# W_G's weight sums in the middle block's W_O, column sums by transposition, and four smaller edits to a one-core layer kernel

## The chip, the core and the metric

The kernel runs on one core of one Trainium2 chip. The core has five engines, each with an in-order queue of its own: TensorE (PE; its weight loads are listed as PEld), VectorE (DVE), ScalarE (ACT), GpSimd (POOL) and SyncE (SP), which here only issues transfers. Sixteen DMA engines carry all transfers, whether SP or POOL issued them. The metric is the device time of one execution, in microseconds. Before the change it is 2609.93, the median of three runs (2609.04 to 2610.62).

## What is computed

One layer over 2048 prompt tokens and 64 decode tokens, 1024 wide. The projections go into a short convolution (path A) and a recurrence over 8 heads in chunks of 64 tokens (path B); both are gated, merged and multiplied by `w_o`; a norm, a residual, another norm and a gate follow. Cut to what matters:

```python
h = rms_norm(x, g_pre)
vA, bA, cA, zA, q, f, iv, zB, gA, gB = split_cols(einsum('btd,dn->btn', h, w_in))
u = cA * vA
yA = einsum('btc,cd->btd', silu(zA) * bA * causal_conv3(u_ext, conv_w), w_a_out)
S_new, o = hgrn2_scan(S0, silu(q) * QK_SCALE, 1 - fg, iv, log(fg))   # chunks of 64
yB = einsum('btc,cd->btd', rms(o) * g_onorm * silu(zB), w_b_out)
out = einsum('btd,de->bte', sigmoid(gA) * yA + sigmoid(gB) * yB, w_o)
x = x + rms_norm(out, g_post)
gate = sigmoid(einsum('btd,de->bte', rms_norm(x, g_ple), w_ple_gate))
x = x + einsum('btp,pd->btd', p, w_ple_proj) * gate
```

`rms_norm` divides each token by the root of the mean of its squares over the 1024 features. All is fp32.

## The kernel before

**Layout.** Features lie on the 128 partitions, tokens along the free axis. The 2112 tokens are cut into three blocks of 704 (`BN`), each of two halves of 352 (`HN`). A feature row block is a tile of 128 x 704 from one ring of 52 such buffers (`RING`, tag "r", `rt()`); half tiles come from nine "hf" buffers (`hf()`). The ring serves almost everything: x, operands, heads, outputs, weights that are being summed. PSUM has five banks for gemms and three for the rest.

**Arithmetic.** Each fp32 operand is split into a high half (a cast on ScalarE, `split`) and a low half (a subtraction on VectorE), and each product takes three matmuls: high by high, high by low, low by high (L363 to L365 in `sgroup`, L496 to L498 in `in_turn`, L529 to L531 in `mm3`). A weight block of 128 x 512 needs a raw buffer (5), a high buffer (4, tag "hi", `split_w`) and a low one (4 "lo" or 3 "s"). Low halves that were made once are kept in DRAM and loaded again.

**Seven products.** Pairs of output row blocks are computed for both token halves with seven products of block sums instead of eight (`PRODUCTS`, `sgroup`); the weights need four sums, S1 to S4, for each pair. In block 0 they are made as needed (`combined`, L297). For W_A, W_B, W_O and W_G `prepare_sums` makes them ahead: for each of four pairs POOL loads four blocks into ring tiles, VectorE makes four sums (L337 to L343), ScalarE and VectorE split them, and POOL stores the sums and their low halves (L326, L329), to be loaded again by SP when they are used. The token side needs sums too (`operands`: x is loaded by POOL at L643, scaled at L693, summed at L675 to L678 and split).

**Order.** The framework lays out each engine's queue at compile time by priority and readiness as it estimates them, except where `issue_after`, `high_priority` or a "hook" says otherwise. `hooks` is a list of small steps: after each of the seven products of a group (and each half gemm) one is taken, so that a head's attention (`head_attn`, four steps per part, three parts) or a norm (`final_norm`) is threaded into the products. An entry None lets a product pass. `spread_out` builds such a list for the norms; it must be used up by the groups that follow (seven groups of seven products).

**Stages of a block.** Gates and path B (eight heads; `path_b`), path A (`path_a`, with `side` running the next block's column norms and a `prepare_sums`), the merge (W_A, W_B), W_O, and the final norm, which runs by hooks inside the next block's first gates. At the end of W_O the next block's operands are made (`ops`, in steps 1, 3, 5 and 7 of `final_out`). The second block's output gate with W_G (`final_gate`) is done inside the last block, for which its rows are stored and loaded again; the last block uses the seven products for W_G as well (`gate_in_turn`), and there W_G's sums are read.

**The norms.** `col_rstd` sums squares over the 128 partitions: for each 128 tokens a matmul with the squares as weights and a column of ones as the moving operand (L620), then scale (VectorE, L591) and power (POOL, L593). `spread` turns the three columns back by transposition against the identity (L604), and a copy takes them out of PSUM (L630).

Of the kernel before, what the change touches and what calls it, by code (L numbers as in the profile page):

```python
# [18 lines left out]
P = 128  # L19
D = 1024  # L20
# [15 lines left out]
CUT = 1344  # L36
BN = 704
HN = BN // 2
NB = TOK // BN
RING = 52  # L40
# [5 lines left out]
def plan():  # L46


    out = []
    for t0 in range(0, TOK, BN):  # L50
        runs, groups = [], []
        for lo, hi, sample in ((0, CUT, False), (CUT, CUT + DEC, True), (CUT + DEC, TOK, False)):
            a, b = max(lo, t0) - t0, min(hi, t0 + BN) - t0
# [7 lines left out]
        halves = [dict(t0=t0 + o, off=o, n=HN) for o in (0, HN)]  # L61
        out.append(dict(t0=t0, n=BN, runs=runs, npair=npair, parts=parts, groups=groups, segs=halves, last=t0 + BN == TOK))
# [20 lines left out]
def hybrid_step(  # L83
# [34 lines left out]

    def rt(n=BN, dt=F32):
        t = ring.tile([P, BN + 4], dt, tag="r", name=nm("r"))  # L120
        return t if n is None else t[:, :n]

    def hf(n=HN):
        return ring.tile([P, HN + 32], F32, tag="hf", name=nm("hf"), bufs=HALVES)[:, :n]

# [3 lines left out]
    def ps_gemm():  # L129
        return psg.tile([P, 512], F32, tag="pg", name=nm("pg"))[:, :HN]  # L130

    def spill(kind, j):
        return dram.tile([P, BN], F32, tag=f"{kind}{j}", name=nm(kind), bufs=2)
# [4 lines left out]
    ones = const.tile([P, 1], F32, tag="ones", name="ones")  # L138
    V.memset(ones, 1.0)
# [6 lines left out]
    keep = const.tile([P, BN], F32, tag="keep", name="keep")  # L146
    atts = [
        const.tile([P, max(len(b["parts"][i]) for b in blocks), P], F32, tag=f"att{i}", name=f"att{i}") for i in range(NPART)
# [41 lines left out]
    def split_rt(src):  # L190
        hi, lo = rt(dt=F32R), rt(dt=F32R)
        split(src, hi, lo)
        return hi, lo
# [19 lines left out]
    def split_w(raw, key=None, queue=SP):  # L213

        hi = wp.tile([P, 4, P], F32R, tag="hi", name=nm("hi"))
# [178 lines left out]
    def half(t, h):  # L394
        return t[:, h * HN : (h + 1) * HN]
# [151 lines left out]
    def gemm_late(idxs, act, segs, late):  # L547
# [3 lines left out]
        ks = [k for k in range(KB) if k != late] + [late]  # L551
# [55 lines left out]
    def spread_all(cols):  # L607

        rs = rt()
        for h in range(2):  # L610
            A.copy(half(rs, h), spread(cols[h], HN))
        return rs

    def col_rstd(acc, n):
# [3 lines left out]
        with placed():  # L618
            for i, o in tiles_of(n):
                T.matmul(pc[:, i : i + 1], acc[:, o : o + P], ones, start=True, stop=True)  # L620
        rstd_of(pc[:, : cols.shape[1]], cols, 1.0 / D)
# [19 lines left out]
    def load_x(bl, k):  # L641
        t = rt()
        G.dma_start(t, x_fm[k * P : (k + 1) * P, bl["t0"] : bl["t0"] + BN])  # L643
        return t

    def row_rstd(bl, out):

        out.extend(cols_tile(HN) for _ in bl["segs"])
        todo = [(cols, s["t0"] + o, i) for cols, s in zip(out, bl["segs"]) for i, o in tiles_of(HN)]
# [120 lines left out]
    def path_a(bl, hc, a, first, extra, ready=None):  # L770

        for j in range(KB):
            next(extra, None)
            n = bl["n"]
            pos = [r[0] + 2 * i for i, r in enumerate(bl["runs"])]
            hists = [hist_s if r[2] else hist_p for r in bl["runs"]]
            ct, u, conv = rt(), rt(None), rt()
# [4 lines left out]
            def times_u(h, v):  # L782
                for (o, ln, _), q in zip(bl["runs"], pos):
                    lo, hi = max(o, h * HN), min(o + ln, (h + 1) * HN)
                    if lo < hi:
                        V.tensor_tensor(
                            u[:, q + 2 + lo - o : q + 2 + hi - o], v[:, lo - h * HN : hi - h * HN], ct[:, lo:hi], ALU.mult
# [13 lines left out]
            for (o, ln, _), q, hist in zip(bl["runs"], pos, hists):  # L801
                d = conv[:, o : o + ln]
                A.mul(d, u[:, q : q + ln], cw[0][:, j : j + 1])
                for w in (1, 2):
                    V.scalar_tensor_tensor(d, u[:, q + w : q + w + ln], cw[w][:, j : j + 1], d, ALU.mult, ALU.add)
# [20 lines left out]
    def head_prep(bl, hc, hd, first, hs):  # L826
        n, npair = bl["n"], bl["npair"]
        nch, np1 = n // CH, npair * P
# [18 lines left out]
        qc = small.tile([P, 2, BN // CH], F32, tag="qc", name=nm("qc"))  # L847
        f, r = qc[:, 0, :nch], qc[:, 1, :nch]
        ka, kb, qx, vt, z = hf(HN + 32), rt(), rt(), rt(), rt()

        def scaled(after):
# [16 lines left out]
            two = kb[:, : 4 * P].rearrange("p (c q t) -> p c q t", q=4, t=CH)  # L868
            rest = kb[:, 4 * P : np1].rearrange("p (g c t) -> p g c t", c=2, t=CH)[:, :, 0, :]

            def pairs(x, at):
                return x[:, : 4 * P].rearrange("p (c e h t) -> p c e h t", e=2, h=2, t=CH)[:, :, :, at, :]
# [629 lines left out]
```

## Time and profile before

| | |
|---|---|
| median of 3 runs | 2609.93 us |
| profiled execution | 2611.61 us |
| its span, first to last instruction | 2609.9 us |
| TensorE busy in the span | 2588.6 us |
| TensorE clock granted (mean) | 1.000 |
| bytes moved by DMA | 745.99 MB, 286 GB/s over the span |

In a list of waits a row reads: engine, tile and line that waited, what it waited for, then us in total, times, longest. In the chain of waits a row is start, us, what ran (or was waited for) on the chain that ended last. In the timeline a row is start, duration, engine, line, operation, tiles, shape, and in brackets the idle time before it with what ended it. In a table of stages a row is from:to, length, then busy us and instruction count of PE, PEld, DVE, ACT, POOL, the clock, the DMA share and GB/s. In a list of groups: line, engine, operation, out<-in, shapes, count | busy us, mean ns | idle before. In the list of transfers the last number is the median time in us from issue to landing. TensorE's matmuls overlap, so starts lie closer together than durations: a 352-column matmul is listed with about 0.32 us and the next starts 0.16 us later.

### The profile page before, as it was taken

How to read it: one execution, taken by the hardware profiler on the slowest of the kernel's cores; microseconds unless marked ns; L12 is line 12 of the kernel's file. 1: busy time of each engine (PE TensorE's matmuls, PEld its weight loads, DVE VectorE, ACT ScalarE, POOL GpSimd, SP SyncE). 2: the span in 40 equal slices, each digit the busy share in tenths (PEclk: the TensorE clock that was granted, in tenths of full speed). 3: DMA queues.
4: the chain of work that ended last, by engine and by line, in shares of the span. 5: the costliest groups of instructions: out<-in, count | busy, mean ns of one | idle time of the engine just before them, and what ended most of it. 6: DMA issues, size and time to landing. Idle time of an engine off the chain costs nothing.

```text
span 2609.9 us, 47443 instructions
## 1 busy us (share of the span) xinstructions
PE 2588.6 (99%) x16562; PEld 2572.5 (99%) x16562; DVE 1667.1 (64%) x3232; ACT 1538.9 (59%) x2940; POOL 392.6 (15%) x722
## 2 busy tenths in 40 slices
PE   8999999999999999999999999999999999999999
PEld 8999999999999999999999999999999999999998
DVE  8778888888766555455545568553455544568756
ACT  6666665554434644677745556466667744555746
POOL 2000000200441212101112211021000101210220
PEclk9999999999999999999999999999999999999999
DMA  7687787898988997777789989599776789999977
GB/s 285 234 275 259 251 285 257 306 318 286 342 292 285 351 320 259 248 231 224 226 288 359 381 311 312 193 359 358 229 230 220 224 256 335 377 321 309 339 256 240
DMA packets 362672, 745.99 MB, mean 286 GB/s; under 512 B 44640, under 2 KB 49280, under 8 KB 362432
## 3 DMA queue, kind: packets, MB, share of 16 engines
q1 hardware_dynamic: 319680, 579.55, 65.4%
q0 software_dynamic: 42464, 163.37, 17.0%
q8 instruction: 130, 2.13, 0.3%
q14 instruction: 110, 0.90, 0.1%
q10 hardware_dynamic: 288, 0.05, 0.0%
HBM read 531.74 MB, written 211.04 MB: 285 GB/s over the span
## 4 chain that ended last, share of the span: by engine, by line
PE 89%; DMA 3%; DVE 2%; issue 2%; ACT 1%; POOL 1%; DVEq 0%; POOLq 0%; ACTq 0%; SPq 0%
PE pg L363 19%; PE pg L365 19%; PE pg L364 19%; PE pg L496 4%; PE pg L497 4%; PE pg L498 4%; PE pg L530 4%; PE pg L531 4%; PE pg L529 4%; PE pa L994 1%; PE pa L958 1%; PE pa L996 1%; PE pa L944 1%; DMA r<-w_blk 1%; DMA raw<-S 1%
## 5 line engine op out<-in xcount | busy, mean ns | idle before, releaser
L363 PE MATMUL pg<-r,hi 128*128 128x352 f32 x3304 | 1092.9, 331 | 4.6 <-DVE r L409 3.1
L364 PE MATMUL pg<-r,hi 128*128 128x352 f32 x3304 | 1067.6, 323 | 0.0
L365 PE MATMUL pg<-r,lo 128*128 128x352 f32 x2356 | 762.1, 323 | 1.2 <-DMA lo<-low 1.2
L218 ACT CAST hi<-raw 128x512 fp32r<-128x512 f32 x720 | 445.0, 620 | 499.8 <-PE pg L364 165.6
L363 PEld LDWEIGHTS pg<-r,hi 128*128 128x128 f32 x3304 | 622.2, 188 | 9.1 <-DVE r L409 3.2
L364 PEld LDWEIGHTS pg<-r,hi 128*128 128x128 f32 x3304 | 622.2, 188 | 0.0
L365 PEld LDWEIGHTS pg<-r,lo 128*128 128x128 f32 x2356 | 442.3, 188 | 1.8 <-DMA lo<-low 1.7
L365 PE MATMUL pg<-r,s 128*128 128x352 f32 x948 | 306.2, 323 | 0.1
L530 PE MATMUL pg<-r,hi 128*128 128x352 f32 x768 | 248.4, 324 | 0.0
L529 PE MATMUL pg<-r,hi 128*128 128x352 f32 x768 | 248.1, 323 | 0.0
L188 ACT CAST hi<-raw 128x512 fp32r<-128x512 f32 x218 | 134.6, 621 | 153.1 <-PE pg L364 53.5
L188 DVE TENSOR_TENSOR r<-r,r 128x352 fp32r<-128x352 f32 (+3 forms) x298 | 182.8, 637 | 62.7 <-ACT r L188 61.7
L497 PE MATMUL pg<-r,hi 128*128 128x352 f32 x672 | 217.3, 325 | 0.0
L496 PE MATMUL pg<-r,hi 128*128 128x352 f32 x672 | 213.6, 325 | 0.1
L531 PE MATMUL pg<-r,lo 128*128 128x352 f32 x656 | 211.9, 323 | 0.1
L188 ACT CAST r<-r 128x352 fp32r<-128x352 f32 (+3 forms) x298 | 162.2, 580 | 56.9 <-DVE r L1114 15.4
L188 DVE TENSOR_TENSOR lo<-raw,hi 128x512 fp32r<-128x512 f32 x218 | 149.4, 687 | 63.5 <-ACT hi L188 55.2
L365 PEld LDWEIGHTS pg<-r,s 128*128 128x128 f32 x948 | 178.4, 188 | 0.4 <-DMA s<-low 0.4
L188 ACT CAST hi<-s 128x512 fp32r<-128x512 f32 x160 | 98.5, 621 | 123.0 <-PE pg L364 105.8
L377 ACT COPY hf<-pg 128x352 f32<-128x352 f32 x354 | 157.1, 446 | 11.5 <-PE pg L365 10.9
L530 PEld LDWEIGHTS pg<-r,hi 128*128 128x128 f32 x768 | 144.3, 188 | 0.3 <-DVE r L188 0.2
L529 PEld LDWEIGHTS pg<-r,hi 128*128 128x128 f32 x768 | 144.2, 188 | 0.0
(367 smaller groups left out, 4157.0 us busy)
## 6 DMA issues: line engine op xcount, KB each, us to landing
raw<-w_blk SPq DMA_DIRECT2D x570, 256.0 KB, 4.2
lo<-low SPq DMA_DIRECT2D x411, 256.0 KB, 4.4
raw<-S SPq DMA_DIRECT2D x408, 256.0 KB, 4.4
low<-lo SPq DMA_DIRECT2D x314, 256.0 KB, 3.7
s<-low SPq DMA_DIRECT2D x309, 256.0 KB, 4.2
S<-s SPq DMA_DIRECT2D x152, 256.0 KB, 3.2
r<-w_blk POOLq DMA_DIRECT2D x64, 256.0 KB, 7.3
S<-r POOLq DMA_DIRECT2D x64, 256.0 KB, 5.8
```

Source lines behind the costliest of these rows:

```text
L188: return A.copy(hi, src).ins, V.tensor_tensor(lo, src, hi.bitcast(F32), ALU.subtract).ins
L218: A.copy(hi, raw)
L363: add(hi[:, k, :], xhi, start=start and k == 0, stop=False)
L364: add(hi[:, k, :], xlo, start=False, stop=False)
L365: last[0] = add(lo[:, k, :], xhi, start=False, stop=k == KH - 1).ins
L377: copied = A.copy(got[n], ps[bank])
L496: add(hi[:, k, :], xhi, start=start and k == 0, stop=False)
L497: add(hi[:, k, :], xlo, start=False, stop=False)
L498: last[0] = add(lo[:, k, :], xhi, start=False, stop=k == KH - 1).ins
L529: T.matmul(ps, hi[:, k % 4, :], xhi[:, c], start=k == ks[0], stop=False)
L530: T.matmul(ps, hi[:, k % 4, :], xlo[:, c], start=False, stop=False)
L531: last[0] = T.matmul(ps, lo[:, k % 4, :], xhi[:, c], start=False, stop=k == ks[-1]).ins
```

## The change

- `prepare_sums((W_G,), ...)` runs in the middle block, in steps 0, 2, 3, 4 and 5 of `final_out` (the first only loads), and no longer in the last block's `path_a`.
- `col_rstd` transposes the squares (three transposes into PSUM) and lets VectorE add up along the free axis; the column of ones goes.
- The high halves of weights have five buffers instead of four; the ring has 51 tiles instead of 52.
- The last block's two half norms share their three working tiles and load x once, in whole rows.
- `final_gate` keeps the sigmoid in half tiles, multiplies in place and loads x in the step that uses it.
- One more empty hook before the last attention step of block 0's first head; in `spread_out` for the first two blocks' norm one more empty hook before each spreading and one fewer behind the last row of the norm's first pass.
- `gemm_late` takes k in the order late+1, ..., late (mod 8) instead of 0, 1, ... with `late` at the end.
- Block sizes come from a list, `SIZES = (704, 704, 704)`. The blocks, their halves and the attention's parts stay as they were; the helpers take the width from the current block (`wide`, `width_of`, `of_block`).

The core of the diff, without the edits that only rename widths:

```diff
-RING = 52
+RING = 51
...
-        hi = wp.tile([P, 4, P], F32R, tag="hi", name=nm("hi"))
+        hi = wp.tile([P, 4, P], F32R, tag="hi", name=nm("hi"), bufs=5)
...
-        ks = [k for k in range(KB) if k != late] + [late]
+        ks = [(late + 1 + k) % KB for k in range(KB)]
...
             for i, o in tiles_of(n):
-                T.matmul(pc[:, i : i + 1], acc[:, o : o + P], ones, start=True, stop=True)
-        rstd_of(pc[:, : cols.shape[1]], cols, 1.0 / D)
+                T.transpose(pc[:, i * P : i * P + P], acc[:, o : o + P], ident)
+        nt = cols.shape[1]
+        V.tensor_reduce(cols, cols3(pc, nt), axis=mybir.AxisListType.X, op=ALU.add)
+        rstd_of(cols, cols, 1.0 / D)
...
-                    hooks.append(None)
+                    hooks.extend([None] * (2 if first and hd == 0 else 1))
...
-    def final_norm(bl, segs, xo, acc, h2, kept, raw=False):
+    def final_norm(bl, segs, xo, acc, h2, kept, raw=False, common=None):
+        common = {} if common is None else common
+        if not common:
+            common.update(tiles=[rt(), rt(), rt()], xks=[])
...
-        acc2, rs, rs2 = rt(), rt(), rt()
-        xks = []
-        def fetch():
-            j = len(xks)
-            if j < KB:
-                xks.append(rt())
-                G.dma_start(xks[j][:, c], x_fm[j * P : (j + 1) * P, segs[0]["t0"] : segs[0]["t0"] + n])
-        for _ in range(3 if bl["last"] else 4):
-            fetch()
+        (acc2, rs, rs2), xks = common["tiles"], common["xks"]
+        ahead = 3 if bl["last"] else 4
+        def fetch(upto):
+            while len(xks) < min(upto, KB):
+                xks.append(load_x(bl, len(xks)))
+        fetch(ahead)
...
     def final_gate(bl, segs, h2, kept, queue=G):
-        def fetch(j):
-            return [reload(kept[kind, j]) for kind in "xp"] if j < KB else None
-        nxt = fetch(0)
+        nxt = reload(kept["p", 0])
         for j in range(KB):
+            pj, xj = nxt, reload(kept["x", j])
             pss = gemm(W_G + j, h2, segs)
-            (xj, pj), nxt = nxt, fetch(j + 1)
-            t = rt()
+            nxt = reload(kept["p", j + 1]) if j + 1 < KB else None
             for s, ps in zip(segs, pss):
-                A.activation(t[:, cols_of(s)], ps, AF.Sigmoid)
-            V.tensor_tensor(t, pj, t, ALU.mult)
-            V.tensor_tensor(t, t, xj, ALU.add)
+                gate = hf()
+                A.activation(gate, ps, AF.Sigmoid)
+                V.tensor_tensor(pj[:, cols_of(s)], pj[:, cols_of(s)], gate, ALU.mult)
+            V.tensor_tensor(pj, pj, xj, ALU.add)
...
-        sums_ahead = prepare_sums((W_A, W_B), True) if first else prepare_sums((W_O,) if nxt else (W_G,), False)
+        sums_ahead = prepare_sums((W_A, W_B), True) if first else prepare_sums((W_O,), False) if nxt else iter(())
+        gate_sums = prepare_sums((W_G,), False) if nxt and not first else iter(())
...
             for j, _ in enumerate(final_out(segs, mg, xo, acc, KB - 1 if first else KH - 1)):
+                if j in (0, 2, 3, 4, 5):
+                    next(gate_sums, None)
                 if j in (1, 3, 5, 7):
                     run(ops, 1)
...
-            spread_out((norm, (0, 1, 0, 1) + (0, 1, 0) * KB + (0, 1, 0, 1) + (0, 1) * KB))
+            spread_out((norm, (0, 1, 0, 0, 1) + (0, 1, 0) * (KB - 1) + (0, 1) + (0, 1, 0, 0, 1) + (0, 1) * KB))
```

170 lines of the change are left out of this document (97 added, 73 removed).

## The prediction

> **What bounds the kernel now.** I read the page first (busy time, clock), then who TensorE waited for, then a table of stages, then the chain of waits and the timeline at the places that the change touches.
>
> ```profile
> span 2609.9 us, 47443 instructions
> PE 2588.6 (99%) x16562; PEld 2572.5 (99%) x16562; DVE 1667.1 (64%) x3232; ACT 1538.9 (59%) x2940; POOL 392.6 (15%) x722
> PEclk9999999999999999999999999999999999999999
> ```
>
> TensorE (PE) is busy for 99% of the span, at the full clock in every slice. Only two kinds of gain are left: TensorE work taken out, and the 21 us (2609.9 - 2588.6) in which it idles. What it waited for, in total, times and longest, in us:
>
> ```profile
> PE pa L1058 <- ACT r L188: 6.6, 1, 6.6
> PE pg L363 <- DVE r L409: 3.1, 9, 0.6
> PE pa L1008 <- DVE r L1003: 1.7, 1, 1.7
> PE pg L363 <- ACT hi L218: 1.5, 2, 0.7
> PE pg L365 <- DMA lo<-low: 1.2, 1, 1.2
> ```
>
> The first is the start of the program, which the change leaves. The second, third and fourth are what three of its edits aim at, 6.3 us together. The fifth, one late weight, isn't addressed. So no edit can bring much, and each is counted in single microseconds.
>
> **Column sums by transposition.** `col_rstd` runs 14 times: twice at the start, then four times for each block. Today each sends 3 matmuls against a column of ones, which appear as 6 TensorE instructions (84 in all); afterwards 3 transposes, such as L604 already runs. The chain of waits shows both, as start, us, what:
>
> ```profile
> 858.00 1.44 PE pa L620 x12
> 862.12 0.66 PE pa L604 x6
> 906.99 1.23 PE pa L620 x12
> 1705.02 1.47 PE pa L620 x12
> 1752.76 1.23 PE pa L620 x12
> 2455.18 0.56 PE pa L620 x6
> ...
> 2485.12 0.56 PE pa L620 x6
> 2509.59 0.80 PE pa L620 x6
> ```
>
> These rows, with a third one of 0.56 left out, are the twelve calls of the three final norms (x12 is two calls, one for each half): 1.44 + 1.23 + 1.47 + 1.23 + 3 x 0.56 + 0.80 = 7.85 us. Six transposes take 0.66, so 0.11 each; 12 x 3 x 0.11 = 3.96. That is **-3.9 us**, on a TensorE with nothing idle around it. The two calls at the start are taken at nothing: there VectorE sets the pace (below). The ends are -3.4 (0.80 and the two 1.4s contain waits that stay) and -4.6 (the start gains its 0.7 too).
>
> ```profile
> L604 PE MATMUL pa<-ident,cols x54: 270/272/324, 24.3 to 2514.2; 128*128 128x128 f32 x54
> ```
>
> This row gives 0.272 us as the duration of a transpose by itself; 0.11 holds only where the next one starts inside it. [...]
>
> Each call also gains a VectorE reduction over 128x384, 14 in all:
>
> ```profile
> L1001 DVE TENSOR_REDUCE ms<-r 128x4 f32<-128x512 f32 x24 | 16.5, 686 | 30.5 <-ACT r L1000 30.5
> 25.18 0.53 DVE L1354 COPY r<-pa 128x352 f32<-128x352 f32 x1 [0.58 <-PE pa L604]
> ```
>
> 384/512 of 0.686 is 0.51 us. In the two norms of the first two blocks it is covered, because the list of hooks gets one more empty step between the sums and the spreading: one product, 12 matmuls, 1.9 us. In the last block the next step comes a whole half-gemm later (24 matmuls, 3.9 us). At the start two of them, 1.0 us, meet 0.58 us of idle VectorE, and the transposes end 0.7 us sooner. So nothing; if the cover is gone, 0.5 us each, 14 x 0.5 = 7 us at most.
>
> **Spread later.** In the first head of the first block the transposition at L1008 comes before VectorE has finished L1003 (start, us, what):
>
> ```profile
> 124.32 0.63 DVE r L1003
> 125.08 0.63 PE pa L1008 x4
> 125.71 0.16 PE pg L365
> 127.45 0.30 PE pa L1008
> ```
>
> 1.7 us of idle (the row of waits above), 0.63 instead of 4 x 0.11 for the restart, and 0.3 more at 127.45, where the second part's transposition arrives early as well. One more empty hook puts L1008 behind 12 further matmuls, 12 x 0.16 = 1.9 us; the data is there at 124.95. **-2.2 us**; ends -2.2 and -1.0 (VectorE, in a queue of its own order, slips with it). What follows, the store of that head's z, comes a product later, and its reader is block 0's merge, after all eight heads.
>
> **A fifth buffer for high halves.** The first group of gates of a block interleaves four products by k, and so holds four high halves until its end. The fifth product's cast can't start before:
>
> ```profile
> 850.04 0.17 PE pg L365
> 850.58 0.63 ACT hi L218
> 851.26 0.43 PE pg L363
> ```
>
> It happens twice (the row of waits). Each costs 0.74 us of idle plus 0.27 (0.43 - 0.16) of restart. With a fifth buffer the cast is done during the four products. **-2.0 us**; ends -2.0 and 0 (if the cast stays queued on ScalarE behind the copy that precedes it). Six of the nine waits of L363 for L409 are in block 0, one in each of six heads, and this is the first:
>
> ```profile
> 180.40 0.43 PE L363 MATMUL pg<-r,hi 128*128 128x352 f32 x1 [0.25 <-DVE r L409]
> ```
>
> There VectorE's low halves for the sums stand ahead of the copy that frees a PSUM bank. ScalarE casts one product earlier with the fifth buffer, so VectorE's order there may change either way: 0, ends -3.1 (six of 0.25 + 0.27) and +1.5 (six idle times doubled).
>
> **W_G's sums.** They leave the middle of the last block and enter W_O of the middle block: 16 loads, 16 sums, 16 splits and 32 stores. The stages (us, PE, PEld, DVE, ACT, POOL, clock, DMA share, GB/s):
>
> ```profile
> 1340.00:1510.00 170.00, 169.40 (x1053) 169.13 (x1053) 86.30 (x170) 94.11 (x196) 41.59 (x93) 1.00 0.99 358
> 1596.00:1698.00 102.00, 101.47 (x627) 99.76 (x625) 60.71 (x112) 54.95 (x110) 6.44 (x12) 1.00 0.67 231
> 2130.00:2290.00 160.00, 158.98 (x985) 158.46 (x985) 75.75 (x125) 78.76 (x150) 27.94 (x58) 1.00 0.98 346
> ```
>
> The second row is where they go, the third where they come from; the first has W_O's own sums. In the third, TensorE twice waits behind VectorE, which waits for the weights loaded by POOL and then does three sums ahead of the copy that TensorE needs:
>
> ```profile
> 2198.71 9.26 DMA r<-w_blk
> 2210.86 0.69 DVE r L343
> 2211.55 0.44 DVE r L409
> 2212.13 0.40 PE pg L363
> 1677.62 1.07 POOL L643 DMA_DIRECT2D r<-x_fm  x2 [28.36 <-PE pg L531]
> ```
>
> Of the 3.1 us in nine waits, six of 0.25 belong to block 0; the three left, 1.6 us, are 0.53 each, and 0.24 of restart (0.40 - 0.16) makes 0.77. Two of them are W_G's: -1.5. In the new place VectorE gets 32 operations of 0.69, 22 us on 60.7 of 102; ScalarE 16 casts of about 0.63, 10 us; POOL 48 issues of 0.54 (half of the L643 row's 1.07), 26 us on 6.4; and the DMA 48 x 262 KB = 12.6 MB, 123 GB/s on 231, which makes 354, as full as the first row, where TensorE still lost only 0.6 us. In W_O ScalarE, not VectorE, frees the PSUM banks, so a VectorE held up by a late load doesn't stop TensorE at once. I charge one wait of 0.77 (ends 0 and four, one for each group, 3.1). Net **-0.7 us**. Behind the waiting VectorE and POOL stand the next block's operands; that is the first rival.
>
> **The edits at nothing.**
>
> ```profile
> r<-x POOLq DMA_DIRECT2D x16, 352.0 KB, 5.4
> ```
>
> In the second block's output gate (run in the last block) x is no longer loaded one step ahead: it lands in 5.4 us and has a gemm of 48 x 0.16 = 7.7 us for it; without that cover, 8 steps would wait up to 5 us each, which only a queue standing on POOL would do. The gate is a half tile, so one VectorE product becomes two halves, off the path. The last norms load each row block once in 352 KB instead of twice in 176 KB: the same bytes. The new order of k in W_O puts the rows that come last, last; the row of waits has none for W_O's lines, so nothing is there to gain.
>
> **Sum**: -3.9 - 2.2 - 2.0 - 0.7 = **-8.8 us**. The profiled execution took 2611.6 us in all, 1.7 outside its span, and becomes 2602.8. It stands 1.7 above the median of 2609.93, so the median becomes **2601 us** (-0.34%).
>
> **The rivals.**
> 1. *Late operands: slower.* The last quarter of the third block's operands already waits 28 us for a ring tile, in the L643 row above, and is made last:
>
> ```profile
> 1702.18 0.89 DVE L188 TENSOR_TENSOR r<-r,r 128x704 fp32r<-128x704 f32 x1 [1.10 <-ACT r L188]
> r<-w_blk POOLq DMA_DIRECT2D x64, 256.0 KB, 7.3
> S<-r POOLq DMA_DIRECT2D x64, 256.0 KB, 5.8
> ```
>
> Its last split ends at 1703, at the end of the new block's first group of gates, whose last products read it, so there is little to spare. The ring loses a tile (52 to 51) and lends W_G 8 to 12. If one group of sums still holds tiles and POOL's queue when these two loads should go, they slip by one group's turn: a load (7.3), eight VectorE operations (5.5) and the landing of the last store (5.8), 18.6 us, and TensorE stops at about 1700 for it: -8.8 + 18.6 gives 2620. It makes the kernel slower from 8.8 us of lateness on, measurably from 14. For it: the 28 us wait on the ring, an idle queue that now fills. Against: the four groups run in steps 0 to 5 of W_O, and the loads wait for step 6, when the first operands of W_O die.
> 2. *Only the work taken out counts.* The waits reappear next to where they were (a new order of casts, one ring tile fewer), and only the -3.9 stays, perhaps with new waits of 1 us: 2606. For it: nine of the waits are for a VectorE that is behind, and the change gives VectorE more to do. Against: each wait has one named cause, which the edit removes.
> 3. *Block 0 gains too.* The six waits go (-3.1): 2598. For it: their chain runs through a cast that waited for a high buffer. Against: the low halves still have four.
> 4. *Transposes don't overlap.* At 0.272 each, 36 cost 9.8 instead of 7.85: +2.0 in place of -3.9, 2607. For it: the duration. Against: six in 0.66 us.
>
> **How the numbers follow.** Forecast 0.45, rival 1 0.13, rival 2 0.20, rival 3 0.18, rival 4 0.04. What can be told from no change is 0.2%, 5.2 us: faster is below 2604.7. Forecast and rival 3 are faster, 0.63; rivals 2 and 4 are the same, 0.24; rival 1 is slower, 0.13. The range: below, rival 3 with the start's 0.7 and the whole of W_G's 0.8 gives 2596, and I leave 1; above, it takes in rivals 2 and 4 and a rival 1 of half its price, 2601 + 9: 2595 to 2611. The forecast's own range is 2598 to 2605.
>
> **What would show it.** Right: 42 transposes at L620's place with 0.66 us for six; TensorE's waits without L1008 <- L1003 and L363 <- ACT hi L218; no wait for L409 after 2130 us; W_O's stage with VectorE near 82 us and DMA share above 0.9; TensorE's busy time near 2585. Wrong: a wait of TensorE for VectorE or ScalarE operands between 1690 and 1710, waits for a spread column (L630), or new waits for weights in W_O.

## The result, and the profile after

The kernel after takes 2654.02 us (median of 4 runs, 2652.41 to 2658.3) against 2610.27 for the kernel before on the same chip (4 runs): ratio 1.017, 95% interval 1.0153 to 1.0188. It is slower by 44 us; 8.8 us less had been forecast, and the time lies above the range. From the page of the kernel after: the span, the busy times, then TensorE and its clock in 40 slices.

```profile
span 2651.3 us, 47374 instructions
...
PE 2592.6 (98%) x16520; PEld 2573.9 (97%) x16520; DVE 1672.0 (63%) x3261; ACT 1536.9 (58%) x2940; POOL 387.9 (15%) x714
...
PE   8999999999999999999999999689999999999999
...
PEclk9999999999999999999999999899999999999999
```

TensorE has 42 instructions fewer (16562 before) but is busy 4 us longer, and one place, slices 26 and 27 (1657 to 1789 us), holds nearly all of its new idle time. To place it exactly I compared the start of the n-th matmul after with the n-th before, the column sums left out: the program's other matmuls are the same in number. How far the difference grows in each stretch (us, on the clock of the kernel before):

```
                     0-60 100-150 800-910 1600-1660 1660-1710 2100-2350 2440-2530   all
after                +1.1    +1.5    -2.1      +4.5     +35.4      -1.7      +2.8  +41.3
```

The last column is the whole program. 39.9 of 41.3 us are lost between 1600 and 1710, in the middle block's W_O and the first gates of the next block, where W_G's sums now stand. The 4.5 us before 1660 are four short waits for splits at the start of W_O (2.0 us together) and slow matmuls behind them (starts 0.29 us apart instead of 0.16). What TensorE waited for in the kernel after (total, times, longest):

```profile
PE pg L549 <- ACT r L1185: 16.3, 1, 16.3
PE pg L382 <- ACT r L207: 11.3, 1, 11.3
...
PE pa L624 <- POOL cols L613: 3.7, 5, 2.5
PE pg L382 <- DVE r L429: 3.3, 7, 0.5
...
PE pa L1034 <- DVE r L1029: 2.0, 1, 2.0
```

(Lines of the kernel after: L549 is L529 of before, L382 L363, L1185 L1159, L207 L188, L1034 L1008, L1029 L1003, L429 L409, L624 L604. Left out are the start's wait, as before, and others of up to 2.3 us.) Two waits are new and large: one at the end of W_O for ScalarE's copy out of PSUM, one in the first gates for a cast of an operand. What stands behind the copy is seen in the timelines of the kernel after, first POOL's: start, duration, what was issued, and in brackets the idle time before it and what ended it.

```profile
1621.74 0.54 POOL L339 DMA_DIRECT2D r<-w_blk  x1 [0.22 <-issue]
1622.72 1.06 POOL L665 DMA_DIRECT2D r<-x_fm  x2 [0.44 <-PE pg L518]
1655.47 0.54 POOL L345 DMA_DIRECT2D S<-r  x1 [31.69 <-DVE r L356]
...
1687.75 0.54 POOL L665 DMA_DIRECT2D r<-x_fm  x1 [0.32 <-issue]
...
1720.28 1.07 POOL L665 DMA_DIRECT2D r<-x_fm  x2
```

The first group's blocks are asked for at 1622, but the first store of a sum waits until 1655 for VectorE, and the x of the operands' second pair (L665), issued at 1627 before, stands behind the stores of two groups and goes at 1687.75; the third pair goes at 1720 (before, even the fourth and last pair went at 1677). Now VectorE:

```profile
1654.50 0.68 DVE L356 TENSOR_TENSOR r<-r,r 128x512 f32<-128x512 f32 x1
...
1678.13 0.69 DVE L356 TENSOR_TENSOR r<-r,r 128x512 f32<-128x512 f32 x1 [8.17 <-DMA r<-w_blk]
...
1693.36 0.69 DVE L356 TENSOR_TENSOR r<-r,r 128x512 f32<-128x512 f32 x1 [9.18 <-DMA r<-w_blk]
...
1695.43 0.95 DVE L715 SCALAR_TENSOR_TENSOR r<-r,vec,r 128x704 f32<-128x704 f32 x1
...
1713.30 0.69 DVE L356 TENSOR_TENSOR r<-r,r 128x512 f32<-128x512 f32 x1 [6.81 <-DMA r<-w_blk]
...
1726.18 0.95 DVE L715 SCALAR_TENSOR_TENSOR r<-r,vec,r 128x704 f32<-128x704 f32 x1 [7.00 <-DMA r<-x_fm]
```

Each group begins with the sum L356: at 1654.5, 1678.1, 1693.4 and 1713.3, so one every 15 to 24 us, because its loads are issued only after the group before. From the second group on VectorE waits for them, with the operands' scaling (L715) queued behind; the first sum had its blocks, but stood behind a sum of squares of W_O's rows. And ScalarE:

```profile
1674.55 0.45 ACT L1185 COPY r<-pg 128x352 f32<-128x352 f32 x1
...
1696.41 0.49 ACT L207 CAST r<-r 128x352 fp32r<-128x352 f32 x1 [12.43 <-DVE r L715]
...
1701.54 0.80 ACT L1185 COPY r<-pg 128x352 f32<-128x352 f32 x2
```

A cast that waits 12.4 us for VectorE stands ahead of the copies that empty the PSUM banks. The banks fill, and TensorE stops, for 16.3 us. The chain reads: load of W_G's block, its sum on VectorE, the operand behind it on VectorE, that operand's cast on ScalarE, the copy behind the cast, TensorE; POOL, VectorE, ScalarE and TensorE each work in order, and each is held by the one before. The table of stages of the kernel after (from:to, length, PE, PEld, DVE, ACT, POOL, clock, DMA share, GB/s):

```profile
1650.00:1685.00 35.00, 35.00 (x219) 35.00 (x219) 19.29 (x29) 18.58 (x33) 10.45 (x20) 1.00 0.77 256
1685.00:1702.00 17.00, 0.76 (x5) 0.47 (x3) 8.49 (x14) 3.09 (x6) 6.20 (x12) 0.60 0.77 281
1702.00:1716.00 14.00, 13.97 (x77) 13.97 (x78) 6.68 (x11) 7.65 (x15) 4.61 (x9) 0.88 0.66 221
1716.00:1740.00 24.00, 8.77 (x36) 7.36 (x34) 13.84 (x22) 7.42 (x16) 7.72 (x15) 0.64 0.67 243
```

No engine but TensorE is near full, and the DMA share is 0.66 to 0.77 (0.77 in the forecast's own stretch, 1596 to 1698, where "above 0.9" stood). Nothing is short of throughput; all wait in turn. The clock column brings something else, told at the end.

### The profile page after: what moved, and what is told of

Its sections match the earlier page's. It is cut to its first block, busy times and chain, and to the rows that moved or that the text cites. A ratio compares the mean times of both kernels' runs of the same rounds, so it can differ in the third digit from the quotient of the medians.

```text
span 2651.3 us, 47374 instructions
## 1 busy us (share of the span) xinstructions
PE 2592.6 (98%) x16520; PEld 2573.9 (97%) x16520; DVE 1672.0 (63%) x3261; ACT 1536.9 (58%) x2940; POOL 387.9 (15%) x714
## 4 chain that ended last, share of the span: by engine, by line
PE 86%; issue 5%; DMA 3%; DVE 2%; POOL 1%; ACT 1%; SPq 0%; POOLq 0%; DVEq 0%; ACTq 0%
PE pg L382 19%; PE pg L384 19%; PE pg L383 19%; PE pg L549 4%; PE pg L551 4%; PE pg L550 4%; PE pg L516 3%; PE pg L517 3%; PE pg L518 3%; PE pa L984 1%; PE pa L1020 1%; PE pa L1022 1%; PE pa L970 1%; DMA r<-w_blk 1%; PE pa L1034 1%
## 5 line engine op out<-in xcount | busy, mean ns | idle before, releaser
L382 PE MATMUL pg<-r,hi 128*128 128x352 f32 x3304 | 1095.4, 332 | 18.1 <-ACT r L207 11.3
L384 PE MATMUL pg<-r,lo 128*128 128x352 f32 x2356 | 762.7, 324 | 0.2 <-DMA lo<-low 0.2
L382 PEld LDWEIGHTS pg<-r,hi 128*128 128x128 f32 x3304 | 623.5, 189 | 22.7 <-ACT r L207 11.8
L384 PEld LDWEIGHTS pg<-r,lo 128*128 128x128 f32 x2356 | 443.2, 188 | 0.6 <-DMA lo<-low 0.6
L384 PE MATMUL pg<-r,s 128*128 128x352 f32 x948 | 307.0, 324 | 1.0 <-DMA s<-low 1.0
L549 PE MATMUL pg<-r,hi 128*128 128x352 f32 x768 | 250.3, 326 | 17.4 <-ACT r L1185 16.3
L207 ACT CAST hi<-raw 128x512 fp32r<-128x512 f32 x218 | 134.4, 620 | 152.5 <-PE pg L383 59.8
L207 DVE TENSOR_TENSOR r<-r,r 128x352 fp32r<-128x352 f32 (+3 forms) x298 | 182.1, 635 | 59.5 <-ACT r L207 58.3
L551 PE MATMUL pg<-r,lo 128*128 128x352 f32 x656 | 211.7, 323 | 0.0
L207 ACT CAST r<-r 128x352 fp32r<-128x352 f32 (+3 forms) x298 | 161.9, 578 | 75.8 <-DVE r L715 29.8
L207 DVE TENSOR_TENSOR lo<-raw,hi 128x512 fp32r<-128x512 f32 x218 | 149.0, 686 | 52.4 <-PE pg L551 23.9
L384 PEld LDWEIGHTS pg<-r,s 128*128 128x128 f32 x948 | 178.5, 188 | 1.3 <-DMA s<-low 1.3
L396 ACT COPY hf<-pg 128x352 f32<-128x352 f32 x354 | 156.9, 445 | 11.5 <-PE pg L384 10.7
L549 PEld LDWEIGHTS pg<-r,hi 128*128 128x128 f32 x768 | 145.4, 189 | 18.5 <-ACT r L1185 16.6
L207 ACT CAST hi<-s 128x512 fp32r<-128x512 f32 x160 | 98.0, 617 | 103.2 <-PE pg L383 82.9
```

Of the source, the lines that this page charges most:

```text
L207: return A.copy(hi, src).ins, V.tensor_tensor(lo, src, hi.bitcast(F32), ALU.subtract).ins
L382: add(hi[:, k, :], xhi, start=start and k == 0, stop=False)
L384: last[0] = add(lo[:, k, :], xhi, start=False, stop=k == KH - 1).ins
L396: copied = A.copy(got[n], ps[bank])
L549: T.matmul(ps, hi[:, k % 4, :], xhi[:, c], start=k == ks[0], stop=False)
L551: last[0] = T.matmul(ps, lo[:, k % 4, :], xhi[:, c], start=False, stop=k == ks[-1]).ins
```

## The experiments

Columns: time, the time of the kernel before on the same chip, ratio with its 95% interval; the growth of TensorE's lateness is told as in the table above.

**Which edit.** `a1_wg_back`: the kernel after with W_G's sums back in the last block.

```diff
-sums_ahead = ... prepare_sums((W_O,), False) if nxt else iter(())
-gate_sums = prepare_sums((W_G,), False) if nxt and not first else iter(())
+sums_ahead = ... prepare_sums((W_O,) if nxt else (W_G,), False)
...
-                if j in (0, 2, 3, 4, 5):
-                    next(gate_sums, None)
```

> The changed kernel with W_G's sums back in the last block's path A; everything else of the change stays. Theory: the whole loss (41 us between the two traces, +40 of it between 1625 and 1700 us) comes from W_G's sums in W_O, and the other edits together are worth little: 2612 us, between 2606 and 2616, no TensorE wait over 2 us in the middle block's W_O. Rival (one ring tile fewer, or the new order of k in W_O, delays the next block's operands by itself): over 2630.

2616.66 against 2611.62, 1.0018 (1.0008 to 1.0027): 39 of the 44 us are gone, the time is 0.7 above the range expected, and no wait of TensorE between 1600 and 1720 is longer than 0.5 us.

`a2_wg_only`: the reverse edit on the kernel before, nothing else.

```diff
-sums_ahead = ... prepare_sums((W_O,) if nxt else (W_G,), False)
+sums_ahead = ... prepare_sums((W_O,), False) if nxt else iter(())
+gate_sums = prepare_sums((W_G,), False) if nxt and not first else iter(())
...
+                if j in (0, 2, 3, 4, 5):
+                    next(gate_sums, None)
```

> The kernel before with one edit: W_G's sums made in the middle block's W_O, in steps 0, 2, 3, 4, 5. Theory: this edit alone brings the loss: 2645 to 2655 us, with TensorE waits of over 10 us in W_O. Rival (it needs the fifty-first ring tile or the other edits beside it): under 2625.

2650.18 against 2611.62, 1.0147 (1.0132 to 1.0162): +38.6 us from this edit alone, and its waits are those of the kernel after (L529 is the end of W_O, L363 the first gates):

```profile
PE pg L529 <- ACT r L1159: 16.5, 1, 16.5
PE pg L363 <- ACT r L188: 12.0, 1, 12.0
```

So W_G's move is the cause of nearly everything, and the rest of the change costs about 5 us (a1; 2.6 in its trace) instead of bringing 8.1.

**How much of W_G.** `a7_wg_two_groups`: two of the four groups in W_O, two in the last block's path A.

```diff
-                if j in (0, 2, 3, 4, 5):
+                if j in (0, 2, 3):
                     next(gate_sums, None)
...
+        gate_sums = iter(()) if first else prepare_sums((W_G,), False, 2)
...
+        sums_ahead = prepare_sums((W_G,), False, 0, 2)
```

> The changed kernel with two of W_G's four groups in W_O (steps 0, 2, 3) and two in the last block's path A. Theory of the order: the second quarter of the operands still stands behind two groups (a wait of 10 to 17 us stays), the third and fourth don't, 2625 to 2640. Rival (transfers or ring tiles in proportion to the groups): half of the loss, 2635, with both long waits halved.

2633.13 against 2610.98, 1.0085 (1.0072 to 1.0099). Both readings allowed for this time (+18.9 of 41.3 in the trace); the waits tell them apart. One of the two stops remains (13.1 us) and the other is gone, as the order has it; they aren't both halved.

**What in a turn.** `a8_load_ahead`: each group's blocks loaded one group earlier, as `ahead` does for W_A.

```diff
-            if ahead and n + 1 < len(groups):
+            if (ahead or early) and n + 1 < len(groups):
```

> The changed kernel with W_G's next group loaded before the sums of the present one, low halves still in ring tiles (12 tiles at once). Theory of the round trip (VectorE waits 7 to 9 us for each group because its load can only go after the group before): the waits for W_G's loads shrink and 10 us or more come back, under 2644. Theory of the ring: four tiles more are held, the operands' x comes later still, 2654 or more.

2645.14 against 2611.2, 1.0131 (1.0117 to 1.0145): 9 us back, 1 less than expected, though it holds four more ring tiles. VectorE's waits for W_G's loads fall from 24.2 to 1.6 us (three waits to one, between 1610 and 1740), but its waits for x rise from 7.0 to 15.4: x still goes behind the groups' stores on POOL, the second pair at 1682. So the loads are one part of a turn, x behind the stores is another, and ring space isn't what decides in this order.

`c2_transfers_only`: loads and stores only.

```diff
+            if not work:
+                G.dma_start(lows[i1, name], s)
+                return
...
-            V.tensor_tensor(a22, a21, a22, ALU.add)
+            if work:
+                V.tensor_tensor(a22, a21, a22, ALU.add)
```

> The changed kernel with W_G's 16 loads and 32 stores in W_O and none of its sums and splits: the loaded blocks are stored as they are, so W_G's products come out of wrong sums. Theory of the queues (VectorE and ScalarE, in order, wait for W_G's loads, and the operands and the PSUM copies stand behind them): nearly all comes back, 2612 to 2622. Theory of contention (12.6 MB more in W_O): 2640 or more. Between: x for the operands still stands behind the stores on POOL, 2622 to 2640.

2626.54 against 2611.2, 1.0060 (1.0046 to 1.0073). 28 of the 44 us are gone, so most of the loss hangs on the sums and splits. The ring tiles of the low halves go with them, four instead of eight for each group; a8 speaks against ring space as the reason. Of the 15 us that stay, about 5 are the rest of the change (a1). 12 of TensorE's lateness fall between 1600 and 1710, 7.1 of them before 1660, where the loads and stores, which now wait for no sum, come closer together: a row of the table of stages, and one of ScalarE's casts of a weight that waits for its load.

```profile
1640.00:1660.00 20.00, 19.17 (x97) 17.97 (x98) 6.58 (x12) 6.70 (x14) 9.27 (x18) 0.83 1.02 392
...
1683.08 0.62 ACT L237 CAST hi<-raw 128x512 fp32r<-128x512 f32 x1 [5.19 <-DMA raw<-S]
```

The DMA engines are full there (a share of 1.02; 0.55 in the kernel before in the same 20 us), and at 1630 ScalarE waits 3.9 us for another weight. So transfers this close together can cost something by themselves, here at most those 7.1 us. In the kernel after the share is 0.45 in those 20 us, so c2 doesn't tell the transfers' part in its loss. x goes behind the fourth group's loads, which wait 10.4 us for a ring tile, but VectorE never waits for it here.

**Another order, other queues.** `a5_wg_behind_ops`: all of W_G's steps behind the fourth operand step.

```diff
-                if j in (0, 2, 3, 4, 5):
-                    next(gate_sums, None)
                 if j in (1, 3, 5, 7):
                     run(ops, 1)
+                if j == KB:
+                    run(gate_sums)
```

> The changed kernel with all of W_G's sums behind the fourth step of the operands instead of between them. Theory of the order (VectorE and POOL take the sums' steps ahead of the operands' second to fourth quarter, and each group is a round trip of load, sums, stores): the two long waits in W_O go, 2612 to 2625; a wait or two may come in the last block's first gates. Rival (the transfers themselves, 12.6 MB more in W_O and the gates, starve TensorE of weights or x): over 2635.

2662.23 against 2610.98, 1.0196 (1.0182 to 1.0210). W_O is whole again (+0.6 between 1660 and 1710), and one wait in the next block's first gates takes the place of both:

```profile
PE pg L382 <- ACT r L766: 37.6, 1, 37.6
...
1730.73 0.69 DVE L356 TENSOR_TENSOR r<-r,r 128x512 f32<-128x512 f32 x1 [9.19 <-DMA r<-w_blk]
...
1744.22 0.69 DVE L356 TENSOR_TENSOR r<-r,r 128x512 f32<-128x512 f32 x1 [8.25 <-DMA r<-w_blk]
...
1756.40 0.69 DVE L356 TENSOR_TENSOR r<-r,r 128x512 f32<-128x512 f32 x1 [6.88 <-DMA r<-w_blk]
```

Here the turns stand bare: one in 12 to 13.5 us, of which 7 to 9 wait for the loads, with the gates' sigmoids queued behind them.

`a3_x_on_sp` loads the operands' x on SP, in both blocks; `a10_x_on_sp_ahead` does so in the middle block alone, with the loads of a8.

```diff
-                ops = ... operands(hc, spread_all(cols), partial(load_x, nxt))
+                ops = ... operands(hc, spread_all(cols), partial(load_x, nxt, queue=SP))
```

> The changed kernel with the loads of x for the next block's operands issued by SP instead of POOL. Theory that POOL's queue is what delays them (they stand behind stores that wait for VectorE's sums): 30 us or more come back, 2615 to 2625. Theory that ring tiles are what delays them (the loads can't be placed before the sums give up their tiles, on whatever queue): 2640 to 2665, and SP's weight loads may be held up behind them.

> The kernel after, with W_G's next group loaded one turn ahead (as in a8_load_ahead) and, in the middle block's W_O alone, the operands' x loaded by SP instead of POOL (a3_x_on_sp did that in both blocks and lost 18 us in the first). Theory 'transfers': the operands are late because their loads stand on POOL behind stores that wait for sums; then x of the second pair lands before 1650 us, and 15 us or more of a8's 35 come back: 2630 or less. Theory 'turns': VectorE and ScalarE take the groups and the operands in program order, and a group's turn (its loads, sums, splits) is what the operands wait for; then x may land early, and the time stays at 2640 to 2650.

a3: 2668.46 against 2611.62, 1.0219 (1.0204 to 1.0234), the loss in W_O as in the kernel after and 17.6 us more in block 0's. a10: 2644.63 against 2611.06, 1.0127 (1.0112 to 1.0143), as a8. The time is the one expected of "turns", but x didn't land early, so a10 doesn't decide: SP's queue has its own weights to wait for, issues the second pair at 1673.8, and VectorE still waits for it.

```profile
1673.81 1.06 SPq L665 DMA_DIRECT2D r<-x_fm  x2
...
1685.69 0.95 DVE L715 SCALAR_TENSOR_TENSOR r<-r,vec,r 128x704 f32<-128x704 f32 x1 [7.52 <-DMA r<-x_fm]
```

What an early x would have brought stays open.

`a11_casts_on_dve`: the operands' casts in that W_O on VectorE, so that no such cast stands in ScalarE's queue.

```diff
+                    cast[0] = A.copy if first else V.tensor_copy
                     run(ops, 1)
+                    cast[0] = A.copy
```

> The kernel after, with the casts of the operands' splits in the middle block's W_O made by VectorE instead of ScalarE (some 16 casts, about 9 us more on VectorE), so that ScalarE has no instruction there that waits for an operand. Theory 'held copies': TensorE's first stop (16.3 us, L549 for L1185) is nothing but ScalarE's copies out of PSUM standing behind such a cast; then that wait goes, and if it was a cost of its own the time falls by 12 us or more, to 2642 or less. Theory 'late operands': the hold only sets the place; the wait goes from W_O and the same time is waited in the new block's first gates (L382), and the total stays at 2650 to 2662.

2657.88 against 2611.06, 1.0178 (1.0165 to 1.0192). The stops change places and the sum stays (L551 is the end of W_O, L384 the first gates):

```profile
PE pg L384 <- DVE r L209: 17.3, 1, 17.3
PE pg L551 <- ACT r L1187: 12.6, 1, 12.6
...
1704.91 0.81 ACT L1187 COPY r<-pg 128x352 f32<-128x352 f32 x2 [6.12 <-DVE r L209]
```

The copies (L1187) no longer stand behind a cast of an operand, but behind W_G's own casts, and then wait 6.1 us for VectorE all the same: a copy reads PSUM and writes a ring tile, so what it waits for there can only be a tile that VectorE's split of an operand lets go. The rest comes late at the first gates. The cast that held the copies set the place of the loss, not its size.

`a9_pool_sums`: the order of a5 with W_G's sums, casts and subtractions on POOL.

```diff
-            split(s, lo, lo)
+            on.tensor_copy(lo, s)
+            on.tensor_tensor(lo, s, lo.bitcast(F32), ALU.subtract)
...
-            V.tensor_tensor(a22, a21, a22, ALU.add)
+            on.tensor_tensor(a22, a21, a22, ALU.add)
```

> W_G's sums behind the operands' steps, and the additions, casts and subtractions done by POOL, so that only POOL waits for W_G's loads. Theory of the queues: the 38 us wait in the last block's first gates goes, 2612 to 2630; POOL's own work (24 operations of 128x512 for each pair of kinds, price unknown) may hold up the norm's x loads and spills. Rival (the wait is for transfers, not for engines): 2650 or more.

2696.51 against 2611.2, 1.0328 (1.0312 to 1.0344), the worst. A sum takes POOL 1.26 us, nearly twice VectorE's 0.69, and the first sigmoid of the new block waits for a ring tile that only a store of W_G frees:

```profile
1733.97 1.26 POOL L360 TENSOR_TENSOR r<-r,r 128x512 f32<-128x512 f32 x1 [3.46 <-DMA r<-w_blk]
...
1772.25 1.28 ACT L770 ACT_TABLE_LOAD   x1 [49.68 <-DMA S<-r]
```

**Low halves elsewhere.** Both kernels put W_G's low halves into the three "s" buffers that the weights use too; `a6_wg_ahead` also loads ahead.

```diff
-            lo = sum_tile(F32R) if ahead else tile_of(F32R)
+            lo = sum_tile(F32R) if ahead or small_low else tile_of(F32R)
...
-gate_sums = prepare_sums((W_G,), False) ...
+gate_sums = prepare_sums((W_G,), True) ...
```

The first two lines are a4's edit, the last two a6's.

> The changed kernel with the low halves of W_G's sums in the three small buffers of tag s instead of ring tiles, so that a group of sums takes 4 ring tiles instead of 8. Theory of the ring: at least 10 us come back, under 2645. Theory of POOL's queue (same order of loads and stores): within 5 us of 2654.

> The changed kernel with W_G's groups loaded one ahead, as W_A's and W_B's are, and their low halves in the s buffers. Theory of the round trip: VectorE's waits for W_G's loads (8.2, 9.2 and 6.8 us in the changed kernel) shrink, and 10 to 20 us come back, 2634 to 2644. Theory of the ring: a group more of loads takes four more ring tiles, the operands come later still, over 2654.

a4: 2658.23 against 2611.62, 1.0182 (1.0165 to 1.0199). a6: 2653.21 against 2610.98, 1.0163 (1.0147 to 1.0178). Waits for the weights' own low halves take the place of part of the others (10.9 us in a4, 26.7 in a6). So holding fewer ring tiles for W_G brought nothing in this form; what it is worth without those new waits isn't shown.

**The other edits, from the kernel before.** `b1_transpose_only` (`col_rstd` by transposition and the norms' hooks), `b2_hi5_only` (five high buffers, 51 ring tiles), `b3_spread_later_only` (the later step in block 0's first head), `b4_transpose_and_later` (b1 and b3), and b4 with one edit more: `b6_shared_norm` and `b7_gate_in_halves`. The edits are those of the change, each alone; b2's and b3's in full:

```diff
-RING = 52
+RING = 51
...
+        hi = wp.tile([P, 4, P], F32R, tag="hi", name=nm("hi"), bufs=5)
```

```diff
-                    hooks.append(None)
+                    hooks.extend([None] * (2 if first and hd == 0 else 1))
```

> The kernel before with the column sums by transposition and the matching empty hooks of the norms, nothing else. Theory (4.8 us of matmuls go, 3.7 us come back as waits of the spreading for POOL's power, because the reduction lengthens the chain): -1 us, between -3 and +1. Rival (the waits belong to the other edits): -4 us.

> The kernel before with the fifth high buffer and 51 ring tiles, nothing else. Theory (the wait for the fifth product's cast halves twice, -1 us, and block 0's six waits grow by 0.23 us each, +1.4): 0 to +1 us, with the six waits at 0.8 us from start to start as in the changed kernel. Rival (the six waits grew through another edit): -1 us.

> The kernel before, with only the one further empty hook ahead of the last attention step of block 0's first head. If the prediction's term is right, the wait of L1008 for L1003 (1.7 us) is gone and the time is 2.2 us less (ratio 0.9992). If the data slips with the step, as it seems to in the kernel after, a wait of 1.5 to 2 us stays and the time is the same within 0.5 us.

> The kernel before with the column sums by transposition, the norms' hooks and the later step in block 0's first head, with four high buffers, 52 ring tiles and W_G where it was. If the edits add up by the prediction, -3.9 and -2.2: 2605 against 2611 (ratio 0.9977). If what is saved is given back in waits for the power on POOL, as in b1_transpose_only: 2608 to 2611 (0.999 to 1.000).

> b4_transpose_and_later with one more edit: the last block's two half norms share their three working tiles and load x once in whole rows. The kernel after and a1_wg_back lose 2.8 us between 2440 and 2530 us on before's clock, where this norm runs beside the second block's output gate; b1_transpose_only loses nothing there, b4 0.7. If the sharing is the cause, 2 us or more are lost there and the time is 2610 to 2612. If it costs nothing, as the prediction has it: as b4, 2609, and the loss there stays below 1 us.

> b4_transpose_and_later with one more edit: the second block's output gate (run in the last block) loads x in the step that uses it, keeps the sigmoid in half tiles and multiplies in place. If this edit is the cause of the 2.8 us between 2440 and 2530 us (VectorE gets two products of 0.51 for one of 0.89 in each step, and these stand ahead of the norm's squares): 2 us or more are lost there and the time is 2610 to 2612. If it costs nothing: as b4, 2609.

```
                time     before   ratio (95%)               100-150  800-910  2100-2350  2440-2530
b1_transpose..  2609.40  2610.98  0.9995 (0.9986 to 1.0003)    -0.0     -0.6       -1.7       +0.0
b2_hi5_only     2615.66  2611.20  1.0016 (1.0008 to 1.0025)    +2.6     -1.8       -1.1       +0.0
b3_spread..     2608.61  2611.06  0.9991 (0.9982 to 1.0000)    -1.9     -0.3       -0.9       +0.0
b4_transpose..  2608.72  2611.06  0.9991 (0.9982 to 1.0000)    -2.0     +0.2       -1.7       +0.7
b6_shared_norm  2608.80  2611.13  0.9991 (0.9982 to 1.0000)    -2.0     -1.1       -1.7       +1.3
b7_gate_in..    2609.32  2611.13  0.9992 (0.9984 to 1.0001)    -2.0     -2.6       -0.4       +0.3
a1_wg_back      2616.66  2611.62  1.0018 (1.0008 to 1.0027)    +0.1     -1.0       -2.1       +2.8
```

The right half is the growth of TensorE's lateness, as before, from one profiled execution each. b1's waits show what the transposes give back:

```profile
PE pa L604 <- POOL cols L593: 2.0, 5, 0.6
...
PE pa L620 <- DVE r L641: 1.5, 2, 1.0
```

None of the two stood in the kernel before: the spreading now comes before POOL's power is done. b2's timeline in block 0's first head shows where the fifth buffer costs:

```profile
121.25 0.28 ACT L1000 ACTIVATE lone<-pa 64x128 f32<-64x128 f32 x1
121.53 0.60 ACT L1000 ACTIVATE r<-pa 128x512 f32<-128x512 f32 x1
...
127.34 0.63 PE L1008 MATMUL pa<-ident,r 128*128 128x128 f32 x4 [3.12 <-DVE r L1003]
```

ScalarE now squares the one-group part "lone" ahead of the four-group part "r", and TensorE's wait for L1003 is 3.1 us instead of 1.7. The edit touches nothing there; with other counts of buffers the framework lays out ScalarE's queue differently (five high buffers and 51 ring tiles weren't tried apart). In b3, with four buffers, the order is the old one and the wait is gone:

```profile
119.38 0.60 ACT L1000 ACTIVATE r<-pa 128x512 f32<-128x512 f32 x1
120.36 0.27 ACT L1000 ACTIVATE lone<-pa 64x128 f32<-64x128 f32 x1
...
124.48 0.63 PE L1008 MATMUL pa<-ident,r 128*128 128x128 f32 x4
```

No kernel here is faster than the kernel before by more than 0.2%; b3, b4 and b6 are the nearest, 2.3 to 2.5 us below it.

## Why the prediction was wrong

- **W_G's sums, -0.7: this is the step that failed.** "In W_O ScalarE, not VectorE, frees the PSUM banks, so a VectorE held up by a late load doesn't stop TensorE at once. I charge one wait of 0.77" counted engine time and bytes. ScalarE's queue there also holds the operands' casts, which wait for VectorE, so a late load does reach the copies; the operands' x stands on POOL behind the groups' stores; and each of the four groups is a turn of its own (15 to 24 us in W_O, 12 to 13.5 in a row), not a wait of 0.77. The term measured +38.6 us (a2).
- **Rival 1 had the mechanism and too small a price and chance.** Operands late behind W_G's turns, TensorE stopped near 1700: so it came, at 1685 and 1716. It priced one group's turn, 18.6 us, where two stops came to 27.6 and slow matmuls to 4 more. Its counter-argument, that the loads of x wait for step 6 of W_O anyway, was true for the last pair only (1677); the second and third pairs, issued at 1627 to 1649 before, now went at 1688 and 1720. The ring wait that it named isn't what decides (a8), though it shows where the sums or the casts are moved (c2, a9, a11).
- **The -1.5 in path A** came in size (a2, the move alone, loses 1.7 us of lateness there) but can't be credited to the move: b1 and b4, which leave W_G there, lose 1.7 as well, and b2 1.1, and in none of the three is either of the two waits left. They weren't a fixed cost of W_G there.
- **Transposes, -3.9:** the work was right. These are the groups of `col_rstd` in the kernel before and in the kernel after, with busy us and mean ns behind the count:

```profile
L620 PE MATMUL pa<-ones,r 128*128 128x1 f32 x84 | 10.1, 244 | 0.1
```

```profile
L640 PE MATMUL pa<-ident,r 128*128 128x128 f32 x42 | 6.1, 274 | 0.7 <-DVE r L661 0.7
```

That is 4.0 us less for 14 calls, so rival 4 (2 us more) is refuted: it priced each transpose at its duration, but these overlap, and 42 of 274 ns take 6.1 us, not 11.5. The cover was overestimated: b1 as a whole brings 1.6 us (0.9995, zero within its interval), since 2.0 us of waits for POOL's power and 1.5 for VectorE's squares take the place.
- **Spread later, -2.2:** right, alone: in b3 the wait is gone, its trace gains 1.9 us in that stretch, and it is 2.45 us faster as a whole (its interval reaches 1.0000). In the kernel after a wait of 2.0 stays, since with the new counts of buffers the data comes later by as much.
- **Fifth buffer, -2.0:** the waits for L218 go (none in b2's list). What that brings can't be told: the stretch of the first ones, 800 to 910, moves by +0.2 to -2.6 in kernels without the edit. The six waits of block 0, which rival 3 let go, double from 0.25 to 0.49 us each in b2, the bad end that the prediction named. The new layout costs 2.6 in block 0's first head, 1.4 of longer wait and the rest, 1.2, in slow matmuls behind it (starts 0.30 us apart). As a whole b2 is 4.5 us slower than before; its trace is 2.5 longer, the rest stays open. No bound allowed for the new layout: a count of buffers was taken for a local edit.
- **Edits at nothing:** the shared norm and the gate in halves are each within 0.6 us of b4, as forecast. The 2.8 us that the kernel after and a1 lose in the last block's norm hold one wait of 2.4 us for POOL's power (L624 for L613), and belong to neither edit alone; which combination makes them wasn't tried. The new order of k in W_O wasn't run alone.

## What to carry to other kernels

Before moving a block of loads, arithmetic and stores, write down for each in-order queue that it enters who stands behind each of its waits, and price it in turns (load, arithmetic, store, next load), not in engine time: in the stages above no engine but TensorE was over 60% (VectorE 58% at most), the DMA share was 0.66 to 0.77, and 39 us went. An instruction that waits for a late operand, ahead of the copies that free PSUM, set the place where TensorE stopped; taking it out of that queue (a11) brought nothing, since the operands stayed late. And a buffer count is a global edit where a framework lays out the queues: compare the order of instructions in places that the edit doesn't touch.

## What the hardware showed

Behind some stops TensorE ran slow for a while. The restart at 1702 in the kernel after, as start, duration, line:

```profile
1702.03 0.66 PE L549 MATMUL pg<-r,hi 128*128 128x352 f32 x1 [16.27 <-ACT r L1185]
...
1704.55 0.49 PE L551 MATMUL pg<-r,s 128*128 128x352 f32 x1
1704.84 0.49 PE L549 MATMUL pg<-r,hi 128*128 128x352 f32 x1
...
1706.41 0.32 PE L551 MATMUL pg<-r,s 128*128 128x352 f32 x1
1706.57 0.32 PE L549 MATMUL pg<-r,hi 128*128 128x352 f32 x1
```

For 3.4 us matmuls start 0.29 us apart, then 0.16; the granted clock is 0.50 up to 1705.41 and 0.88 over the stage from 1702 to 1716. Between 1600 and 1760 us 32 starts are so spaced in the kernel after and none in the kernel before: 32 x 0.13 = 4.2 us on top of the stops. The clock of the kernel after falls from 1.00 to 0.50 at 128.45, 1640.56, 1688.34 and 1719.06, which lie 443, 14 and 9 times 3.4133 us apart, though TensorE's stops before them began at 126.23, 1636.68, 1685.77 and 1716.35; it stays down for 3.41, 3.41, 17.07 and 17.07 us, once or five times that length. TensorE wasn't idle for all of such a length before a fall. Four stretches, in the columns of the stages:

```profile
125.04:128.45 3.41, 1.40 (x10) 1.14 (x9) 2.48 (x6) 0.97 (x2) 1.60 (x1) 1.00 0.62 231
128.45:131.86 3.41, 3.41 (x14) 3.41 (x13) 3.08 (x10) 0.00 (x0) 1.11 (x2) 0.50 0.34 110
...
1637.15:1640.55 3.40, 1.87 (x7) 1.11 (x8) 3.25 (x8) 1.75 (x4) 0.00 (x0) 1.00 0.30 92
1640.56:1643.97 3.41, 3.41 (x13) 3.41 (x13) 0.14 (x1) 0.00 (x0) 0.00 (x0) 0.50 0.27 82
```

TensorE was busy for 1.40 us of the first and 1.87 of the third, and half clock followed both. The first holds a stop of 2.3 us (nine starts 0.29 us apart behind it); the third only the four short waits at the start of W_O, 2.0 us together. In a1 a stop of 2.3 us in the same place (125.25 to 127.58 from start to start) has starts 0.16 us apart behind it. Behind the 3.1 us wait of b2 they are 0.30 apart again (128.06, 128.36). So in these runs a stop, or a few short ones, cost about 1.4 us beyond its length (4.2 us for the three slow stretches after 1600) or nothing; what decides between the two can't be told from them.
